# Value products of both query halves issued together, in parts of 256 columns

## The chip, the cores and the metric

The kernel runs on one core of a Trainium2 chip. The metric is the device time of one execution in microseconds. Before the change it is 2518.14 us, the median of three runs (2516.71 to 2518.36). Everything is computed in 32-bit floats: either plain fp32, or fp32r operands split by hand into an exact high part and the rest.

## The reference

A two-layer generator works on 1024 latent tokens and 256 context tokens of width 1024. Each layer modulates the stream, projects it once, feeds three groups of heads (a bidirectional recurrence, grouped attention, neighbourhood attention), gates and projects the result and normalises it. What the change touches is the attention of the two last groups, cut to what matters:

```python
# grouped attention: 6 query heads, 2 key heads, head width 64, all 256 + 1024 keys
s = jnp.einsum('bqgrd,bsgd->bgrqs', qi, keys)
p = jax.nn.softmax(s, axis=-1)
o = jnp.einsum('bgrqs,bsgd->bqgrd', p, vals)
# neighbourhood attention: 4 heads, the same with a window of 8 x 16 grid cells,
# a learned bias on the scores of the window, and all context keys in the same softmax
```

In layer 0 the context tokens attend too (to the 256 context keys); layer 1 leaves them out.

## The kernel before

`layer_proj` computes the projections of a layer, calls the recurrence (`rwkv`, through `mid`) and then the last projections; `attention(l)` comes behind it in the text, and `out_proj` behind that. The program is built with a planner (`schedule_with_timeline_sim=True`, L1369): it decides, while the program is built, in which order each engine gets its instructions, from what is ready in its own model of the run and from the order of the text. On the chip every engine then takes its instructions in that fixed order. So the recurrence, which is earlier in the text, and the attention are interleaved on all engines.

The recurrence is a serial chain of 40 steps in each layer (`wave_chain`): small matmuls at L704, a copy on ScalarE (L710), matmuls at L715, copies (L721), matmuls at L725, a product on VectorE (L730), and the next step. L630 copies a wave's transposed tiles on ScalarE, 16 copies a wave.

Attention goes head by head in pairs of loops that run side by side: `pair_main` of the current head and `pair_max` of the next. `pair_max` computes the scores of the next head once (L863, tile `sm`) and reduces each row to its maximum on VectorE (L865). `pair_main` computes the scores again, transposed, with keys on the partitions and 512 queries along them, minus the maximum (L920, L921, tile `st`, two buffers), takes their exponential on ScalarE (L927, tile `pt`, three buffers for each half) and multiplies it with the values (L909). A head has two jobs, the two halves of its 1024 queries. A step of the loop over `g` takes one key tile of 128 keys for both halves; a head of the grouped attention has ten steps. In the neighbourhood heads a step can see 256 or 384 queries, some of the other half (`split`), and a bias is added on VectorE before the exponential (L929).

A value product has 128 keys as its contraction and 64 output rows. So both halves fit side by side into TensorE's columns: half 0 has the column tile at 0, half 1 that at 64 (`tile_position=(0, 64 * i)`), and both accumulate in one PSUM tile `y` of 128 x 512, which has one buffer. Sums over keys are kept by adding the exponentials up on GpSimd and VectorE (L934). `weigh` issues the value products of the step before, kept in `todo`, behind the scores of the current step in the text. Each fp32 value product shows in the trace as two records of the same shape, one behind the other.

At the end of a head `ys` (L954) copies `y` out, the sums are inverted and the result is written to `yg_d`, which the output projection (L1141 to L1143) reads; the output blocks of the recurrence (`out_block`, L761 to L787) write there too.

## Time and profile before

| | |
|---|---|
| median of three runs | 2518.14 us |
| the profiled execution, from its first to its last instruction | 2517.7 us |
| TensorE busy | 2289.5 us, 91% |
| VectorE busy | 1669.4 us, 66% |
| GpSimd busy | 1188.4 us, 47% |
| ScalarE busy | 979.5 us, 39% |
| value products, L909 | 784 records, 343.6 us busy |

PE is TensorE's matmuls, PEld its weight loads, DVE VectorE, ACT ScalarE, POOL GpSimd, SP the queue that issues most DMAs. A row of the timeline merges neighbours of one engine that have the same line and tiles: it has the start, the length of the whole, and behind the shape the number of records (x2 is one value product, x4 two of them). A record's end is modelled and overlaps the next start; what an instruction takes from TensorE is therefore read from its start to the start of the next row. [...]

The stretches used here: neighbourhood heads from 560 to 822 us (layer 0) and 1823 to 2046 us (layer 1), grouped heads from 822 to 1197 us and 2046 to 2388 us.

### The profile page before, as it was taken

The page shows a single profiled execution, that of the slowest core. Times are in us where ns is not written, and L with a number is a line of the kernel's source. Part 1 is how long each engine was busy: PE and PEld are TensorE (multiplying, and loading weights), DVE is VectorE, ACT ScalarE, POOL GpSimd, SP SyncE. Part 2 cuts the span into 40 slices and gives each one's busy share as a digit, 9 for nine tenths or more (in the row PEclk, how much of TensorE's full clock was granted, in tenths as well). Part 3 has the DMA queues.
Part 4 walks back from the last instruction along what each step waited for, and adds up shares of the span by engine and source line. Part 5 has one row for each costly group of instructions (what it writes and reads, how often), then busy time and mean ns, then how long its engine had stood idle before and what let it go on. Part 6 is the DMA issues. An engine that isn't in the chain of part 4 may idle for free. (4 is left out here: it accounts for less than half of the span.)

```text
span 2517.7 us, 56578 instructions
## 1 busy us (share of the span) xinstructions
PE 2289.5 (91%) x22008; PEld 1601.3 (64%) x22008; DVE 1669.4 (66%) x3183; ACT 979.5 (39%) x2074; POOL 1188.4 (47%) x1438
## 2 busy tenths in 40 slices
PE   6989999978898999999899999999778889999887
PEld 3878798765455554544887777887555554544387
DVE  5685524647878878665387885445478797786646
ACT  3433413333544444444233444133344444454422
POOL 4454425344555544453355465344455545544443
PEclk9999999997889999999999999999789898999999
DMA  7355325455555444441332546245645443332332
GB/s 276 117 167 169 106 80 137 101 139 115 123 117 124 104 109 102 114 140 54 104 98 95 159 143 199 87 97 138 154 105 123 101 96 97 83 80 64 112 110 95
DMA packets 448236, 298.09 MB, mean 118 GB/s; under 512 B 249600, under 2 KB 395880, under 8 KB 446944
## 3 DMA queue, kind: packets, MB, share of 16 engines
q1 hardware_dynamic: 439936, 281.71, 41.0%
q0 software_dynamic: 7392, 10.28, 1.5%
q8 instruction: 173, 2.83, 0.5%
q10 hardware_dynamic: 640, 2.49, 0.4%
q14 instruction: 95, 0.78, 0.1%
HBM read 198.37 MB, written 91.79 MB: 115 GB/s over the span
## 5 line engine op out<-in xcount | busy, mean ns | idle before, releaser
L204 PE MATMUL pj<-hlo,wh 128*128 128x512 f32 (+1 forms) x1072 | 400.7, 374 | 14.0 <-DVE hlo L480 7.9
L203 PE MATMUL pj<-hhi,wh 128*128 128x512 f32 (+1 forms) x1072 | 402.9, 377 | 9.8 <-ACT qr L348 5.9
L205 PE MATMUL pj<-hhi,wl 128*128 128x512 f32 (+1 forms) x1072 | 398.9, 373 | 0.2 <-POOL wl L169 0.2
L909 PE MATMUL y<-pt,v 128*64 128x512 f32 (+3 forms) x784 | 343.6, 570 | 0.0
L865 DVE TENSOR_REDUCE mx<-sm 128x1 f32<-128x512 f32 (+1 forms) x372 | 200.5, 555 | 85.4 <-PE sm L863 83.3
L169 POOL TENSOR_TENSOR wl<-wf,wh 128x512 fp32r<-128x512 f32 x104 | 142.9, 1378 | 205.8 <-ACT wh L168 181.8
L204 PEld LDWEIGHTS pj<-hlo,wh 128*128 128x128 f32 x1072 | 204.2, 191 | 55.3 <-DVE hlo L480 8.2
L203 PEld LDWEIGHTS pj<-hhi,wh 128*128 128x128 f32 x1072 | 203.9, 191 | 55.5 <-ACT qr L348 7.2
L927 ACT ACTIVATE pt<-st 128x512 f32<-128x512 f32 (+1 forms) x292 | 166.7, 583 | 179.4 <-PE st L921 176.9
L205 PEld LDWEIGHTS pj<-hhi,wl 128*128 128x128 f32 x1072 | 204.0, 190 | 37.2 <-issue 2.9
L863 PE MATMUL sm<-k,q 128*128 128x256 f32 (+2 forms) x436 | 167.2, 427 | 20.8 <-DVE mx L865 13.6
L920 PE MATMUL st<-q,k 128*128 128x512 f32 (+3 forms) x376 | 166.8, 447 | 18.3 <-DVE pt L929 6.2
L863 PEld LDWEIGHTS sm<-k,q 128*128 128x128 f32 x436 | 80.3, 203 | 151.8 <-DVE mx L865 41.6
L1141 PE MATMUL pj<-yh,wh 128*128 128x256 f32 x576 | 161.2, 291 | 15.9 <-ACT yh L1115 11.8
L934 POOL TENSOR_TENSOR acc<-acc,pt 128x512 f32<-128x512 f32 x80 | 107.0, 1337 | 138.1 <-ACT pt L927 137.6
L1142 PE MATMUL pj<-yl,wh 128*128 128x256 f32 x576 | 164.4, 288 | 1.0 <-POOL yl L1116 0.9
L1143 PE MATMUL pj<-yh,wl 128*128 128x256 f32 x576 | 162.8, 287 | 0.0
L921 PE MATMUL st<-q,k 65*128 65x512 f32 (+3 forms) x376 | 147.7, 396 | 1.8 <-issue 1.1
L909 PEld LDWEIGHTS y<-pt,v 128*64 128x64 f32 x784 | 72.0, 143 | 104.8 <-issue 94.1
L616 DVE TENSOR_TENSOR G<-gt,msk 64x192 f32<-64x192 f32 (+1 forms) x320 | 110.3, 345 | 39.4 <-PE gt L611 28.0
L920 PEld LDWEIGHTS st<-q,k 128*128 128x128 f32 x376 | 74.8, 200 | 93.8 <-ACT pt L927 28.1
L699 POOL MEMSET X<- 32x192 f32 x320 | 81.7, 255 | 108.8 <-PE ch L742 84.5
(276 smaller groups left out, 5126.5 us busy)
## 6 DMA issues: line engine op xcount, KB each, us to landing
wf<-win SPq DMA_DIRECT2D x104, 256.0 KB
wm<-wmod SPq DMA_DIRECT2D x32, 512.0 KB
yf<-yg_d SPq DMA_DIRECT2D x72, 128.0 KB
wt<-wm SPq DMA_DIRECT2D x8, 1024.0 KB
gate_d<-o SPq DMA_DIRECT2D x32, 256.0 KB
wf<-wout SPq DMA_DIRECT2D x16, 512.0 KB
ldkk<-rw_d SPq DMA_DIRECT2D x40, 192.0 KB
ldkd<-rw_d SPq DMA_DIRECT2D x40, 192.0 KB
```

Of the source, the lines that this page charges most:

```text
L203: nc.tensor.matmul(out=ps[:, :n], lhsT=wh, rhs=hhi[:, k, t0:t0 + n], start=(k == 0), stop=False)
L204: nc.tensor.matmul(out=ps[:, :n], lhsT=wh, rhs=hlo[:, k, t0:t0 + n], start=False, stop=False)
L205: nc.tensor.matmul(out=ps[:, :n], lhsT=wl, rhs=hhi[:, k, t0:t0 + n], start=False, stop=(k == KT - 1))
L863: nc.tensor.matmul(out=sp_[:, :o], lhsT=q[0][:, qc:qc + 128], rhs=k[0][:, c0:c0 + o], start=True, stop=True)
L865: nc.vector.tensor_reduce(out=mx[:, n_:n_ + 1], in_=sp_[:, :o], op=ALU.max, axis=AX.X)
L909: nc.tensor.matmul(out=o, lhsT=v[:, t, :], rhs=p_, start=start, stop=stop and n_ >= len(mm) - 2, tile_position=(0, 64 * i))
L920: nc.tensor.matmul(out=o, lhsT=k[0][:, 128 * t:128 * t + 128], rhs=q[0][:, qa:qb], start=True, stop=False)
L921: nc.tensor.matmul(out=o, lhsT=k[1][0:65, 128 * t:128 * t + 128], rhs=q[1][0:65, qa:qb], start=False, stop=True)
L927: nc.scalar.activation(out=pt[:, :w], in_=sp_[:, :w], func=AF.Exp)
L1141: nc.tensor.matmul(out=p_, lhsT=wh[m][:, k], rhs=yh, start=(x_ == 0), stop=False)
L1142: nc.tensor.matmul(out=p_, lhsT=wh[m][:, k], rhs=yl, start=False, stop=False)
L1143: nc.tensor.matmul(out=p_, lhsT=wl[m][:, k], rhs=yh, start=False, stop=(x_ == KT - 1))
```

## The change

`weigh` no longer sorts the products of a step by half. It makes two lists, one for each half (column tile), cuts each product into parts of at most 256 columns, and issues the lists in turns: first part of half 0, first part of half 1, second part of half 0, and so on. A second edit gives the first of these products a dependency, for the planner's order alone (no semaphore), on the last score product of the second half in the current step (`follow`). The flags that open and close an accumulation are set for each half. Docstrings and comments are dropped.

```diff
+    def follow(ins, prev):
+        tc.add_manual_dep(ins.ins, prev.ins.name, mybir.DependencyInfo(mybir.DependencyClass.NoSync, mybir.DependencyReason.DATA), reason="order")
...
-            todo = []
+            todo, after = [], []
...
             def weigh(stop=False):
-                mm = []
-                for i, first, pt, tiles in todo:
-                    for x_, (t, cc, _) in enumerate(tiles):
+                lanes = [[], []]
+                for x_ in range(max(len(u[3]) for u in todo)):
+                    for i, first, pt, tiles in todo:
+                        t, cc, _ = tiles[x_]
                         if cc is None:
-                            mm.append((x_, i, t, y[64 * i:64 * i + 64, :nq], pt[:, nq * x_:nq * x_ + nq], first and x_ == 0))
+                            src = [(i, 0, nq, nq * x_)]
                         else:
-                            mm += [(i != h, h, t, y[64 * h:64 * h + 64, lo - 512 * h:hi - 512 * h], pt[:, lo - cc[0]:hi - cc[0]], first) for h, lo, hi in split(*cc)]
-                mm.sort(key=lambda u: u[:2])
-                for n_, (_, i, t, o, p_, start) in enumerate(mm):
-                    nc.tensor.matmul(out=o, lhsT=v[:, t, :], rhs=p_, start=start, stop=stop and n_ >= len(mm) - 2, tile_position=(0, 64 * i))
+                            src = [(h, lo - 512 * h, hi - 512 * h, lo - cc[0]) for h, lo, hi in split(*cc)]
+                        for h, c0, c1, p0 in src:
+                            for a0 in range(c0, c1, 256):
+                                a1 = min(a0 + 256, c1)
+                                lanes[h].append((t, pt, a0, a1, p0 + a0 - c0, first and not lanes[h]))
+                order = []
+                for n_ in range(max(len(z) for z in lanes)):
+                    order += [(i, n_) + z[n_] for i, z in enumerate(lanes) if n_ < len(z)]
+                for n_, (i, at, t, pt, a0, a1, p0, start) in enumerate(order):
+                    mm = nc.tensor.matmul(out=y[64 * i:64 * i + 64, a0:a1], lhsT=v[:, t, :], rhs=pt[:, p0:p0 + a1 - a0], start=start,
+                                          stop=stop and at == len(lanes[i]) - 1, tile_position=(0, 64 * i))
+                    if n_ == 0 and after:
+                        follow(mm, after.pop())
                 todo.clear()
+                after.clear()
...
-                        nc.tensor.matmul(out=o, lhsT=k[1][0:65, 128 * t:128 * t + 128], rhs=q[1][0:65, qa:qb], start=False, stop=True)
+                        mm = nc.tensor.matmul(out=o, lhsT=k[1][0:65, 128 * t:128 * t + 128], rhs=q[1][0:65, qa:qb], start=False, stop=True)
...
-                weigh()
+                    after.append(mm)
+                if todo:
+                    weigh()
```

## Rows read from the trace of the kernel before

**Rows 1.** The page's first and fourth parts: busy time of the engines, and the two lines of the chain that ended last.

```profile
PE 2289.5 (91%) x22008; PEld 1601.3 (64%) x22008; DVE 1669.4 (66%) x3183; ACT 979.5 (39%) x2074; POOL 1188.4 (47%) x1438
...
PE 23%; DVE 11%; DMA 6%; issue 3%; ACT 2%; POOL 2%; SPq 1%; DVEq 0%; POOLq 0%; ACTq 0%
...
PE y L909 4%; PE sm L863 2%; PE pj L203 1%; PE pj L204 1%; PE pj L205 1%; PE st L920 1%; PE pj L1141 1%; PE pj L1143 1%; PE pj L1142 1%; DMA yf<-yg_d 1%; DVE G L616 1%; PE st L921 1%; PE ch L725 1%; DMA ls_d<-G 1%; DMA x_d<-s 1%
```

**Rows 2.** Busy time by stretch, grouped heads of layers 0 and 1, then neighbourhood heads of layers 0 and 1. Behind the length: busy us (records) of PE, PEld, DVE, ACT, POOL; granted clock; DMA share and GB/s.

```profile
822.00:1197.00 375.00, 363.54 (x3965) 181.18 (x3962) 268.61 (x595) 171.63 (x386) 174.94 (x200) 0.97 0.39 104
2046.00:2388.00 342.00, 322.10 (x3615) 158.14 (x3615) 256.29 (x547) 156.36 (x340) 168.07 (x194) 0.97 0.34 88
560.00:822.00 262.00, 221.33 (x3143) 137.92 (x3132) 209.66 (x552) 119.97 (x293) 134.49 (x187) 0.85 0.53 122
1823.00:2046.00 223.00, 186.59 (x2843) 115.88 (x2839) 183.01 (x503) 100.56 (x238) 120.02 (x167) 0.88 0.47 106
```

**Rows 3.** The same for the value products (L909) alone: busy us (records) of PE and PEld, and the clock and DMA of the stretch.

```profile
822.00:1197.00 375.00, 134.76 (x280) 26.24 (x280) 0.97 0.39 104
2046.00:2388.00 342.00, 120.77 (x240) 21.50 (x240) 0.97 0.34 88
```

**Rows 4.** What TensorE waited for in the two stretches of grouped heads, longest first (layer 0, then layer 1 after the dots): us in total, times, longest.

```profile
PE kt L626 <- DVE tt L680: 2.3, 1, 2.3
PE ls L951 <- DVE acc L934: 2.1, 1, 2.1
...
PE sm L863 <- DVE mx L865: 3.7, 5, 1.4
PE ch L715 <- ACT rsb L710: 3.0, 3, 1.7
```

**Rows 5.** Timeline of TensorE at the end of layer 0's last grouped head, where nothing else is on it.

```profile
1191.56 1.07 PE L909 MATMUL y<-pt,v 128*64 128x512 f32 x2
1192.56 0.50 PE L920 MATMUL st<-q,k 128*128 128x512 f32 x1
1192.89 0.39 PE L921 MATMUL st<-q,k 65*128 65x512 f32 x1
1193.21 1.07 PE L909 MATMUL y<-pt,v 128*64 128x512 f32 x2
1194.22 0.50 PE L920 MATMUL st<-q,k 128*128 128x512 f32 x1
1194.56 0.39 PE L921 MATMUL st<-q,k 65*128 65x512 f32 x1
1194.88 1.08 PE L909 MATMUL y<-pt,v 128*64 128x512 f32 x4
1195.88 0.63 PE L951 MATMUL ls<-acc,onec 128*32 128x256 f32 x4
```

**Rows 6.** Timeline around the first and the last case at the full clock in which two products of 512 columns, one of each half, stand next to each other and start together (at either clock the grouped heads have 14 of these: 3 in layer 0, 11 in layer 1); PEld rows are the weight loads.

```profile
1110.45 0.20 PEld L909 LDWEIGHTS y<-pt,v 128*64 128x64 f32 x4 [0.38 <-issue]
1110.46 1.08 PE L909 MATMUL y<-pt,v 128*64 128x512 f32 x4
...
1111.47 0.27 PE L876 MATMUL mt<-c_ident,nm 128*1 128x128 f32 x1
...
2338.96 1.08 PE L909 MATMUL y<-pt,v 128*64 128x512 f32 x4
...
2339.97 0.41 PE L951 MATMUL ls<-acc,onec 128*32 128x256 f32 x2
```

**Rows 7.** Timeline of TensorE at two steps of neighbourhood heads in which both halves see 384 queries: uncut (four records of 384 columns), and cut by the boundary between the halves into parts of 256 and 128 columns (eight records).

```profile
731.51 0.87 PE L909 MATMUL y<-pt,v 128*64 128x384 f32 x4
732.30 0.39 PE L863 MATMUL sm<-k,q 128*128 128x256 f32 x1
...
1933.67 0.87 PE L909 MATMUL y<-pt,v 128*64 128x256 f32 x8
1934.47 0.50 PE L920 MATMUL st<-q,k 128*128 128x512 f32 x1
```

**Rows 8.** Timeline of TensorE with a product of 256 columns that stands alone.

```profile
622.62 0.65 PE L909 MATMUL y<-pt,v 128*64 128x256 f32 x2
623.20 0.38 PE L863 MATMUL sm<-k,q 128*128 128x256 f32 x1
```

**Rows 9.** Value products of 512 and of 384 columns in the neighbourhood heads of layer 0, then of layer 1: count | busy us, mean ns | idle.

```profile
L909 PE MATMUL y<-pt,v 128*64 128x512 f32 x32 | 17.2, 618 | 0.0
L909 PE MATMUL y<-pt,v 128*64 128x384 f32 x32 | 13.8, 572 | 0.0
...
L909 PE MATMUL y<-pt,v 128*64 128x512 f32 x32 | 14.8, 645 | 0.0
L909 PE MATMUL y<-pt,v 128*64 128x384 f32 x32 | 12.9, 512 | 0.0
```

**Rows 10.** ScalarE's timeline in layer 1, with an exponential (L927) among copies of the recurrence.

```profile
2245.89 1.29 ACT L630 COPY S<-kt 64x192 f32<-64x192 f32 x4
2247.20 0.60 ACT L927 ACTIVATE pt<-st 128x512 f32<-128x512 f32 x1
...
2248.80 1.28 ACT L630 COPY S<-kt 64x192 f32<-64x192 f32 x4
```

**Rows 11.** The recurrence's first matmuls (L704, 24 records a step) by stretch of layer 1: busy us (records) of PE and PEld.

```profile
1899.00:1974.00 75.00, 2.71 (x120) 1.91 (x120) 0.95 0.52 112
...
2124.00:2199.00 75.00, 2.72 (x120) 1.91 (x120) 0.95 0.35 86
```

**Rows 12.** TensorE's timeline where the recurrence meets little else: the first matmuls of two steps, one behind the other.

```profile
1808.96 0.87 PE L704 MATMUL ch<-X,G 128*32 128x64 f32 x24
...
1818.68 0.87 PE L704 MATMUL ch<-X,G 128*32 128x64 f32 x24 [3.36 <-DVE X L730]
```

**Rows 13.** Weight loads of the value products over the whole span: shortest, median and longest, ns; first and last start.

```profile
L909 PEld LDWEIGHTS y<-pt,v x784: 132/136/233, 584.6 to 2387.0; 128*64 128x64 f32 x196
```

## Prediction

> **What bounds the kernel now.** I read the page first: TensorE is busy 91% of the span, VectorE 66%, and the value products are the largest single line of the chain that ended last, 4% of the span [rows 1]. An average over a whole layer says little about attention, so I cut it into stretches. In the grouped heads TensorE is busy 363.5 of 375 us in layer 0 and 322.1 of 342 us in layer 1, at a granted clock of 0.97, with VectorE at 268.6 and 256.3 us [rows 2]; its longest waits there are 2.3 to 3.7 us in total [rows 4]. There TensorE sets the pace. In the neighbourhood heads it is busy 221.3 of 262 and 186.6 of 223 us, at a clock of 0.85 and 0.88, and VectorE, with 209.7 and 183.0 us, is as loaded [rows 2]: there nobody is alone the bound.
>
> The value products take 134.8 and 120.8 us of TensorE in the two grouped stretches, more than a third of what it does [rows 3]. The reader should look at how they stand. A lone product of 512 columns takes 1.00 us from its start to the next start (1191.56 to 1192.56), and a half step is 0.33 + 0.33 us of scores and this 1.00: 1.66 us, twice for each key tile [rows 5]. Where by chance two products of different halves stand next to each other, both together take 1.00 to 1.01 us: 1194.88 to 1195.88, 1110.46 to 1111.47, 2338.96 to 2339.97 [rows 5, 6]. The two column tiles work at the same time. But the order seldom lets them: 240 records in each grouped stretch (layer 0's other 40 are of context queries, 128 columns wide) are 120 products, 60 possible pairs, and only 3 and 11 pairs stand together. Half 0's scores of the next step become ready when half 0's exponential has freed their buffer, then half 0's product, then the same of half 1.
>
> **The change, part by part.** *Pairing.* Each pair brought together saves 1.00 + 1.00 - 1.01 = 0.99 us of TensorE. Layer 0: 57 x 0.99 = 56.4 us; layer 1: 49 x 0.99 = 48.5 us. In the neighbourhood heads I halve the busy time of the products of 512 and 384 columns, 31.0 us in layer 0 and 27.7 in layer 1 [rows 9]: 15.5, and 12 in layer 1, where a few already stand in pairs. The products of 128 columns I leave out. Together 132 us of TensorE.
>
> *Parts of 256 columns.* They double the products of 512 columns: 136 pairs in the program get two more products for each pair, each with weight loads. Uncut, a pair of 384 columns takes 731.51 to 732.30, 0.79 us; cut into 256 and 128 it takes 1933.67 to 1934.47, 0.80 us [rows 7]. So a pair of four parts costs 1.01 to 1.02 us; I take nothing for the cut. The upper end is a part that stands alone: 0.58 us [rows 8], four of them 2.32 us. The lower end is zero, since no column goes away. The loads themselves (median 136 ns [rows 13]) lie under the running products: four start and end within 0.20 us at the head of a pair that runs 1.08 us [rows 6].
>
> [...]
>
> *The added order.* The first product of a step now stands behind the scores of the next step's second half. Nothing but TensorE's order changes: no DMA and no instruction of SP or GpSimd is moved, and `v` and `pt` are read later, with three buffers of `pt`. What is queued behind is all of TensorE's later work. Does it stall? Let half 1's scores end at T. The pair runs until T + 1.01, half 0's next scores until T + 1.67. Half 1's next scores need half 1's exponential, 0.60 us [rows 10], ready at T + 0.62: 1.05 us to spare. ScalarE, however, runs copies of the recurrence in groups of 1.29 us in front of an exponential [rows 10], and then TensorE waits where before it had half 0's product to do. The bounds of this: nothing, or the excess of 1.29 over 1.05, 0.24 us, at every key step, 120 x 0.24 = 29 us. I don't add it by itself, since the next step counts idle time as a whole.
>
> *From TensorE's time to the span.* With less work, TensorE will wait more for the others. Rows 2 give two kinds of stretch: VectorE's busy time is 0.74 of TensorE's and the stretch is 1.03 of TensorE's (layer 0, grouped), or 0.95 and 1.18 (layer 0, neighbourhood). A line through these has a slope of 0.73; the other two stretches (0.80 with 1.06, 0.98 with 1.20) lie within 0.015 of it. With the savings: grouped layer 0, TensorE 307.1, ratio 0.875, factor 1.131: 347.4 us, 28 less. Layer 1: 273.6, 0.937, 1.176: 321.8, 20 less. Neighbourhood heads: 205.8, 1.02, 1.236: 254.4, 8 less; and 174.6, 1.05, 1.258: 219.6, 3 less. So by the line 48 us in the grouped heads. The other end is that idle time stays as it is: 105 us. I take a quarter of the way from the line to that end, 62 us, because the line's upper points are heads with an addition of VectorE in front of each exponential of the window, which the grouped heads don't have. With 11 us of the neighbourhood heads: 73 us. The profiled span is 2517.7, 0.4 below the median of the runs: 2518.1 - 73 = **2445 us**. Own range of this case 2410 to 2470 (60 to 105 with something lost, or 48).
>
> **The rivals.** *A, TensorE stays the bound throughout.* The grouped heads give all of 105 us, and the neighbourhood heads half of 27: 2518 - 118 = 2400. For it: waits of a few us in 375. Against: VectorE would have to be busy 0.84 and 0.87 of the shortened stretches.
>
> *B, the recurrence keeps its pace, or the pairs are broken up by it.* Layer 1's recurrence takes 120 records at L704 in 75 us, five steps, 15 us each, in the neighbourhood heads as in the grouped heads [rows 11], and it ends with attention. If that pace does not quicken, layer 1 gains nothing, and layer 0, whose recurrence ends earlier, its 28 to 40: about 2480. Against: with little else on TensorE a step took 9.7 us (1808.96 to 1818.68) [rows 12], so most of the 15 are queues. The recurrence is earlier in the text, so the planner may also put its matmuls between the four parts; half of the pairs lost gives 2518 - 36 = 2482. That would be the change not doing what it says.
>
> *C, slower: the clock.* Place: both grouped stretches. If waits of the new order make them like the neighbourhood heads, TensorE has a busy share of 0.845 and a clock of 0.85 there (product 0.718), 0.837 and 0.88 in layer 1 (0.736) [rows 2]. The work that is left is 307.1 x 0.97 = 297.9 and 273.6 x 0.97 = 265.4 us at full clock; divided by the products: 415 and 361 us, 40 and 19 longer than now: 2577. It decides the sign where share times clock falls below 297.9 / 375 = 0.79 and 265.4 / 342 = 0.78; now it is 0.94 and 0.91. Nothing in the profile shows so large a fall without VectorE's full load.
>
> *D, the halves don't overlap in the new order.* Four lone parts [rows 8] take 2.32 instead of 2.01 us: 136 x 0.31 = 42 us, 2560. If instead the eight weight loads of a pair were exposed (8 x 0.136 = 1.09 us on top of 1.01, 2.10 us for a pair): 136 x 0.09 = 12 us, 2530. [...] Against both: rows 6 and 7.
>
> **How the numbers follow.** The likeliest case has 0.46, A 0.15, B 0.20, no change (gains and new waits cancel) 0.05, C 0.10, D 0.04. A difference of 0.2%, 5 us, is about what a measurement of this kernel can tell from no change. Faster: 0.46 + 0.15 + 0.20 = 0.81; same 0.05; slower 0.14. The range takes in nearly all of A, B, and no change, and leaves out C, D and the edge of A: 2390 to 2518.
>
> **What would show it.** Right: in the timeline L909 in rows of x8 that run about 1.08 us, about 120 of 120 pairs in the grouped heads, and its busy time near 65 us in each of these stretches; TensorE's time falling by about 50 us in each, its idle share rising to some 10%, its clock above 0.9; the recurrence's steps near 13 us. A shows as idle time unchanged, B as steps still of 15 us, or as L909 rows split by L725 or L704, C as a clock near 0.86 in the grouped heads, D as L909 rows of more than 2 us. The prediction is wrong if the value products' time halves and the grouped stretches shrink by less than 20 us in sum, or if the pairs are not in the timeline at all.

## The result and the profile after

The changed kernel takes 2503.78 us, the median of 18 runs (2485.41 to 2518.45), against 2517.24 us (18 runs) of the kernel before beside it: a ratio of 0.994 [0.9921, 0.9959], 13.5 us or 0.6% faster. The forecast was 2445 us. The sign is right, and the size is 73 us forecast for 13.5 found.

The page of the changed kernel, its busy time of the engines, stands against [rows 1]:

```profile
PE 2204.5 (88%) x22616; PEld 1655.1 (66%) x22616; DVE 1660.7 (66%) x3183; ACT 978.7 (39%) x2074; POOL 1188.3 (47%) x1438
```

and the group of the value products, now L921, from TensorE's groups over the whole span (before: 784 records, 343.6 us at L909):

```profile
L921 PE MATMUL y<-pt,v 128*64 128x256 f32 (+1 forms) x1392 | 221.2, 406 | 2.7 <-ACT pt L943 2.3 <-issue 0.3
```

The change did what it says. The products went from 343.6 to 221.2 us of TensorE, 122.4 us less, with more and shorter records. Yet TensorE's whole busy time fell only from 2289.5 to 2204.5, by 85.0 us: all its other matmuls together take 37.4 us more than before. And the span, 2517.7 before, is 2502.0, so that TensorE's idle time rose from 228.2 to 297.5, by 69.3 us. The whole result is in this sum, -122.4 + 37.4 + 69.3 = -15.7 us of span. A group's busy time takes each record to its modelled end, which overlaps the next start. Counted from each start to the next over both traces, as rows are read here, the products go from 313.2 to 201.0 us and all other matmuls from 1976.3 to 2003.5: the same sum is then -112.2 + 27.2 + 69.3.

Busy time by stretch, in the order of [rows 2] (columns as there; the grouped heads end at 1196 and 2366 us now):

```profile
822.00:1196.00 374.00, 335.27 (x4251) 205.96 (x4252) 268.38 (x607) 173.20 (x392) 171.04 (x197) 0.91 0.41 106
2046.00:2366.00 320.00, 285.90 (x3941) 178.13 (x3941) 255.88 (x559) 156.76 (x344) 167.09 (x198) 0.93 0.37 95
560.00:822.00 262.00, 200.86 (x3252) 138.29 (x3253) 204.31 (x549) 119.41 (x288) 143.74 (x193) 0.85 0.53 124
1823.00:2046.00 223.00, 176.31 (x2842) 117.39 (x2838) 180.29 (x489) 99.06 (x236) 116.53 (x162) 0.85 0.48 108
```

The same stretches for the value products alone, to be read against [rows 3]:

```profile
822.00:1196.00 374.00, 84.15 (x528) 37.68 (x528) 0.91 0.41 106
2046.00:2366.00 320.00, 72.54 (x480) 31.90 (x480) 0.93 0.37 95
560.00:822.00 262.00, 34.73 (x208) 15.22 (x208) 0.85 0.53 124
1823.00:2046.00 223.00, 29.42 (x176) 12.27 (x176) 0.85 0.48 108
```

In the grouped heads the products fell by 50.6 and 48.2 us, in the neighbourhood heads by 13.4 and 9.7 (the same view of the kernel before has 48.1 and 39.1 us there). But layer 0's grouped heads end where they did (1197, now 1196 us). Only layer 1's end earlier, 22 us. Idle time in the two grouped stretches went from 11.5 and 19.9 to 38.7 and 34.1 us, and the granted clock from 0.97 in both to 0.91 and 0.93.

TensorE's timeline of the changed kernel shows the pair itself, first early in the tail of layer 0, then at its end, where nothing else is left (the rows are those of [rows 5]):

```profile
1094.20 1.98 PE L921 MATMUL y<-pt,v 128*64 128x256 f32 x8
1096.11 0.80 PE L867 MATMUL sm<-k,q 128*128 128x512 f32 x1
...
1183.35 1.08 PE L921 MATMUL y<-pt,v 128*64 128x256 f32 x8
1184.36 0.50 PE L936 MATMUL st<-q,k 128*128 128x512 f32 x1
...
1185.49 1.08 PE L921 MATMUL y<-pt,v 128*64 128x256 f32 x8
```

At the end a pair in four parts takes 1.01 us, 1183.35 to 1184.36, and a whole key step for both halves 2.14 us (1183.35 to 1185.49), where it took 1191.56 to 1194.88, 3.32 us [rows 5]. Here the change gives its full gain. At 1094 us the same eight records take 1.91 us, about twice as long: the granted clock of that stretch is 0.50, where it is 1.00 at the end. In both traces it has no other values; "lower level" stands for 0.50 below, and "full" for 1.00. Of the 120 pairs of the grouped heads (60 in each layer) 105 stand unbroken, with nothing between their eight records; most of the others are split into six and two.

Who ends TensorE's waits? Three groups over the whole span, first of the kernel before, then of the changed one; the last part of a row is the idle time just before the group and what ended it:

```profile
L725 PE MATMUL ch<-X,S 128*64 128x64 f32 x1920 | 87.9, 239 | 6.7 <-DVE X L721 5.6 <-DVE nm L870 0.4 <-DVE onec L816 0.4
L626 PE MATMUL kt<-c_ident,kb 128*128 128x128 f32 x240 | 45.4, 304 | 19.5 <-DVE tt L680 17.3 <-ACT S L630 2.2
L876 PE MATMUL mt<-c_ident,nm 128*1 128x128 f32 x360 | 55.1, 301 | 3.3 <-DVE nm L870 2.0 <-DVE mx L865 0.8 <-DVE mx L867 0.5
```

```profile
L725 PE MATMUL ch<-X,S 128*64 128x64 f32 x1920 | 86.0, 242 | 21.1 <-DVE X L721 20.6 <-DVE onec L820 0.4
L626 PE MATMUL kt<-c_ident,kb 128*128 128x128 f32 x240 | 48.9, 322 | 28.1 <-DVE tt L680 25.4 <-ACT S L630 2.4 <-DMA stg<-k_d 0.2
L880 PE MATMUL mt<-c_ident,nm 128*1 128x128 f32 x360 | 56.7, 300 | 17.8 <-DVE mx L869 9.9 <-DVE mx L871 6.0 <-DVE nm L874 1.9
```

The recurrence's L725 waits 21.1 us in place of 6.7 (for the VectorE copy at L721), the transposes at L626 28.1 in place of 19.5, those of the maxima (L876, now L880) 17.8 in place of 3.3. Nearly all of it is ended by VectorE. So is most of the rise in all: over the whole span, the waits of TensorE that VectorE ends go from 116.5 to 173.7 us, 57 of the 69 us. The chain of waits in one stretch, 2046 to 2360 us in layer 1, says the same; shares of the stretch by line, of the kernel before and then of the changed one:

```profile
by line: PE y L909 23.7%; PE sm L863 9.3%; PE st L920 8.7%; PE st L921 6.1%; issue 3.9%; PE ch L725 3.9%; DVE G L616 3.3%; DMA ls_d<-G 2.7%; DMA wf<-wout 2.5%; DVE mx L865 2.5%; DMA lin<-ls_d 2.1%; PE ch L715 2.0%; PE ch L704 2.0%; DVE acc 
```

```profile
by line: issue 7.6%; PE y L921 7.2%; DVE mx L869 4.9%; DMA ls_d<-G 4.8%; PE sm L867 4.4%; DVE acc L950 4.4%; PE st L936 3.5%; DMA yo<-y_d 3.5%; DVE e L646 3.0%; DVE G L616 3.0%; DMA lin<-ls_d 2.8%; PE st L937 2.7%; DMA y_d<-yst 2.3%; DVE tm
```

Before, the first four places are TensorE's, 47.8% of the stretch. After, the four TensorE lines have 17.8%, and maxima (L869), additions (L950), the recurrence's small operations (L646, L616) and its round trips through memory (`ls_d`, `lin`, `yo`, `y_d`) stand among them. No line stands out any more.

### The profile page after: what moved, and what is told of

The parts are those of the page before. It is cut to its first block, busy times and chain, and to the rows that moved or that the text cites. A ratio compares the mean times of both kernels' runs of the same rounds, so it can differ in the third digit from the quotient of the medians.

```text
span 2502.0 us, 57786 instructions
## 1 busy us (share of the span) xinstructions
PE 2204.5 (88%) x22616; PEld 1655.1 (66%) x22616; DVE 1660.7 (66%) x3183; ACT 978.7 (39%) x2074; POOL 1188.3 (47%) x1438
## 4 chain that ended last, share of the span: by engine, by line
PE 47%; DVE 21%; DMA 14%; issue 6%; ACT 5%; SPq 4%; POOL 3%; DVEq 0%; POOLq 0%; ACTq 0%
PE pj L203 5%; PE pj L204 5%; PE pj L205 5%; PE y L921 4%; DMA ls_d<-G 3%; PE sm L867 2%; PE st L936 2%; DVE mx L869 2%; DVE e L646 2%; DMA lin<-ls_d 2%; PE pj L1159 2%; PE st L937 2%; DVE G L616 2%; PE pj L1161 2%; PE pj L1160 2%
## 5 line engine op out<-in xcount | busy, mean ns | idle before, releaser
L203 PE MATMUL pj<-hhi,wh 128*128 128x512 f32 (+1 forms) x1072 | 404.9, 380 | 7.4 <-ACT qr L348 4.7
L203 PEld LDWEIGHTS pj<-hhi,wh 128*128 128x128 f32 x1072 | 205.0, 192 | 52.8 <-issue 7.0
L869 DVE TENSOR_REDUCE mx<-sm 128x1 f32<-128x512 f32 (+1 forms) x372 | 198.9, 553 | 39.2 <-PE sm L867 37.5
L921 PE MATMUL y<-pt,v 128*64 128x256 f32 (+1 forms) x1392 | 221.2, 406 | 2.7 <-ACT pt L943 2.3
L936 PE MATMUL st<-q,k 128*128 128x512 f32 (+3 forms) x376 | 168.0, 451 | 22.6 <-DVE am L110 6.5
L867 PE MATMUL sm<-k,q 128*128 128x256 f32 (+2 forms) x436 | 169.7, 432 | 19.5 <-DVE mx L869 7.8
L921 PEld LDWEIGHTS y<-pt,v 128*64 128x64 f32 x1392 | 97.1, 146 | 96.3 <-issue 66.3
L950 POOL TENSOR_TENSOR acc<-acc,pt 128x512 f32<-128x512 f32 x80 | 104.5, 1306 | 116.5 <-ACT pt L943 109.9
L867 PEld LDWEIGHTS sm<-k,q 128*128 128x128 f32 x436 | 84.8, 210 | 81.6 <-issue 21.0
L616 DVE TENSOR_TENSOR G<-gt,msk 64x192 f32<-64x192 f32 (+1 forms) x320 | 110.5, 345 | 39.6 <-PE gt L611 28.7
L699 POOL MEMSET X<- 32x192 f32 x320 | 82.9, 259 | 93.2 <-PE ch L742 68.8
L630 ACT COPY S<-kt 64x192 f32<-64x192 f32 x320 | 100.4, 314 | 55.4 <-PE ch L725 28.7
```

Of the source, the lines that this page charges most:

```text
L203: nc.tensor.matmul(out=ps[:, :n], lhsT=wh, rhs=hhi[:, k, t0:t0 + n], start=(k == 0), stop=False)
L867: nc.tensor.matmul(out=sp_[:, :o], lhsT=q[0][:, qc:qc + 128], rhs=k[0][:, c0:c0 + o], start=True, stop=True)
L869: nc.vector.tensor_reduce(out=mx[:, n_:n_ + 1], in_=sp_[:, :o], op=ALU.max, axis=AX.X)
L921: mm = nc.tensor.matmul(out=y[64 * i:64 * i + 64, a0:a1], lhsT=v[:, t, :], rhs=pt[:, p0:p0 + a1 - a0], start=start, stop=stop and at == le ...
L936: nc.tensor.matmul(out=o, lhsT=k[0][:, 128 * t:128 * t + 128], rhs=q[0][:, qa:qb], start=True, stop=False)
```

## The experiments

Eighteen kernels were run, each beside the kernel before on the same chip. "Ratio" is always to that.

**The parts of the change: the cut and the order.** First, the changed kernel with parts of 512 columns:

```diff
-                            for a0 in range(c0, c1, 256):
-                                a1 = min(a0 + 256, c1)
+                            for a0 in range(c0, c1, 512):
+                                a1 = min(a0 + 512, c1)
```

> The changed kernel with uncut products (parts of 512 columns), pairs and added order kept. The changed kernel's profile has the gain of TensorE (value products 343.6 to 221.2 us busy) and a span only 16 us shorter. Theory 1 (the recurrence's chain through all queues sets the pace of the interleaved stretches, the cut costs nothing): time as the changed kernel, 2497 to 2510 us. Theory 2 (the four parts and their loads cost what the pairing gains): 30 us or more faster than the changed kernel, below 2475. Value products busy 220 us or less by both.

2498.13 us, ratio 0.9933 [0.9907, 0.9959], products 222.5 us busy. The cut neither costs nor brings anything that can be told from 0.994. Then the changed kernel without the added order:

```diff
-                    if n_ == 0 and after:
-                        follow(mm, after.pop())
```

> The changed kernel without the added order; the parts still alternate. Theory 1 (recurrence sets the pace): within 10 us of the changed kernel, 2494 to 2514 us, although TensorE has the first part of half 0 alone in most steps (value products near 270 us busy, 50 more). Theory 2b (the added order makes TensorE wait for the second exponential and so gives the gain back): 20 us or more faster than the changed kernel, below 2484.

2525.44 us, ratio 1.0042 [1.0018, 1.0067], slower than before. Its value products:

```profile
L921 PE MATMUL y<-pt,v 128*64 128x256 f32 (+1 forms) x1392 | 285.1, 400 | 3.1 <-issue 1.2 <-ACT pt L944 1.0 <-ACT pt L941 0.8
```

285.1 us in place of 221.2: without the order most first parts of half 0 stand alone. In its grouped heads 20 of the 120 pairs stand unbroken (105 in the changed kernel), and most of the others are split into two and six records. The order is a part of the gain, worth 22 us by the medians (2525.4 against 2503.8), 26 by the ratios. Neither theory had expected this: Theory 1 said the same time within 10 us, Theory 2b a faster kernel.

**What pairing is worth with the recurrence out of the way.** In both kernels the recurrence is left out, and zeros are stored in its place:

```diff
     def rwkv(l, lay):
+        if True:
+            with tc.tile_pool(name=f"zf{l}", bufs=1, side="right") as zp:
...
+                for i in range(3):
+                    nc.sync.dma_start(out=yg_d[i], in_=zf)
+            return
```

> The kernel before with the recurrence left out (its gated output is replaced by zeros; its inputs are still projected). It is the base for the next run. TensorE's work of the recurrence in attention (some 200 us in sum) goes, so both theories expect 2200 to 2330 us, with attention stretches bound by TensorE, busy over 0.93.

> The changed kernel with the recurrence left out in the same way. Theory 1 (in the whole kernel the recurrence's chain takes the gain): here the pairing gives most of what was predicted of TensorE, 80 to 130 us less than the kernel before without recurrence. Theory 2 (attention itself doesn't get faster: exponentials, VectorE's maxima and sums or the clock take the gain): less than 40 us less.

2056.61 us without pairing (ratio 0.8182 [0.8151, 0.8212]) and 1934.65 with it (0.7696 [0.7672, 0.7721]): pairing is worth 122 us. Busy time in the attention of layers 0 and 1, columns as in [rows 2], first without pairing, then with it:

```profile
528.00:981.00 453.00, 432.53 (x1863) 190.64 (x1863) 238.71 (x550) 171.24 (x330) 139.53 (x105) 0.93 0.26 69
1560.00:1934.00 374.00, 361.58 (x1288) 148.40 (x1288) 211.06 (x471) 145.88 (x250) 129.07 (x94) 0.98 0.20 53
```

```profile
526.00:905.00 379.00, 354.18 (x2163) 200.37 (x2163) 252.38 (x550) 169.51 (x330) 139.28 (x105) 0.93 0.32 82
1482.00:1808.00 326.00, 302.28 (x1592) 166.67 (x1592) 235.26 (x471) 143.41 (x250) 128.74 (x95) 0.92 0.24 61
```

TensorE is idle 20 and 12 us without pairing, 25 and 24 us with it: here the time that TensorE saves is the time that the kernel saves. So the pairs are right, and it is the company of the recurrence that takes the gain. That company is more than one thing: without the recurrence VectorE too is busy only 53 and 56% of these stretches (238.7 of 453 us, 211.1 of 374), against 75 and 78% with it (the rows of whole attention below).

**Is it the length of the recurrence's serial chain?** Each step copies `rsb` on ScalarE. Moved to VectorE, in both kernels:

```diff
-                nc.scalar.copy(rsb, rs)
+                nc.vector.tensor_copy(rsb, rs)
```

> The changed kernel with one step of the recurrence's chain (the copy rsb, L710) moved from ScalarE to VectorE. In the changed kernel this copy waits 2.2 to 2.6 us a step in ScalarE's queue, and VectorE's wait in the same chain is 0.9 to 1.1 us. Theory 1 (the chain's own length through the queues is the bound of the interleaved stretches): 1.2 us of some 70 steps, 25 to 85 us less than the changed kernel. Theory 3 (the order that the planner fixed, and with it the mixture, is the bound, no single hop): within 12 us of it.

> The same move in the kernel before, where TensorE is busy 97% of the grouped heads. Theory 1: TensorE is the bound there, so the shorter chain gives less than 15 us. Theory 3: within 12 us too.

and the chain made longer, with the copy done twice on ScalarE:

```diff
-                nc.scalar.copy(rsb, rs)
+                rsa = r2.tile([128, 3, 64], F32, tag="rsa", name="rsa")
+                nc.scalar.copy(rsa, rs)
+                nc.scalar.copy(rsb, rsa)
```

> The changed kernel with the chain made longer: rsb is copied twice, one behind the other on ScalarE, about 0.3 us a step and 25 us in 80 steps. Theory 1: 12 to 35 us more than the changed kernel. Theory 3: less than 8 us more, since ScalarE is busy below half.

> The same longer chain in the kernel before. Theory 1: TensorE is the bound, so less of the 25 us shows than in the changed kernel, 0 to 12 us. Theory 3: less than 8 us.

Changed kernel: 2502.46 (0.9968 [0.9947, 0.9989]) with the copy moved, 2494.12 (0.9938 [0.9915, 0.9962]) with it doubled. The kernel before: 2545.16 (1.0139 [1.0111, 1.0167]) and 2532.89 (1.0083 [1.0059, 1.0108]). A longer chain does not slow the changed kernel: the theory that the chain's own length is the bound fell. Something else showed: small edits make the kernel before 0.8 to 1.4% slower, and leave the changed one where it is.

**VectorE relieved.** The largest item of VectorE is the maxima. They were taken over a quarter of the columns, in both kernels:

```diff
-                            nc.vector.tensor_reduce(out=mx[:, n_:n_ + 1], in_=sp_[:, :o], op=ALU.max, axis=AX.X)
+                            nc.vector.tensor_reduce(out=mx[:, n_:n_ + 1], in_=sp_[:, :o // 4], op=ALU.max, axis=AX.X)
...
-                        nc.scalar.activation(out=pt[:, :w], in_=sp_[:, :w], func=AF.Exp)
+                        nc.scalar.activation(out=pt[:, :w], in_=sp_[:, :w], func=AF.Exp, scale=1.0 / 64)
```

> The kernel before, with each row maximum of a score tile taken over the first quarter of its columns (the exponential is scaled by 1/64, so that it stays finite; the values of the output are not the reference's). VectorE loses work and nothing else changes: the reductions of L865, some 0.55 us each now, should come near 0.25 us (the 3-column reduction that follows takes 0.15), about 370 x 0.3 = 110 us of VectorE in the two attention stretches. Theory V (in the changed kernel VectorE's queue is what TensorE waits for; in the kernel before TensorE was the bound in the grouped heads): little here, 0 to 25 us less than before (2492 to 2517). Theory W (not VectorE's load, but the recurrence's preparation, a chain of round trips through all engines and two DMAs, in an order fixed at build time): also little, 0 to 25 us.

> The same edit in the changed kernel. Theory V: now TensorE waits less, and the pairing pays: at least 40 us under the changed kernel (2464 or less), and at least 60 us under the same edit in the kernel before. Theory W: as little as there, and the pair with and without pairing differs by what the three pairs so far differ by, 13 to 43 us.

VectorE's groups in layer 1's attention (busy us, mean ns), first of the changed kernel, then the maxima of this one:

```profile
L869 DVE TENSOR_REDUCE mx<-sm 128x1 f32<-128x512 f32 (+1 forms) x176 | 95.8, 561 | 16.9 <-PE sm L867 16.1
L646 DVE TENSOR_TENSOR e<-e,tmp 128x15 f32<-128x15 f32 (+7 forms) x105 | 36.6, 349 | 1.5
L644 DVE TENSOR_TENSOR tmp<-nn,e 128x15 f32<-128x15 f32 (+7 forms) x105 | 26.9, 256 | 1.7
```

```profile
L869 DVE TENSOR_REDUCE mx<-sm 128x1 f32<-128x128 f32 (+1 forms) x176 | 40.8, 252 | 21.8 <-PE sm L867 20.9
```

A reduction went from 561 to 252 ns. The kernel before became slower, 2544.99 (1.0148 [1.0116, 1.018]); the changed one went to 2455.63 (0.9802 [0.9758, 0.9845]), 35 us under its plain form by the ratios. Now pairing is worth 89 us by the medians, 87 by the ratios. This is beyond the 13 to 43 of Theory W, and over the 60 that Theory V asked for. But 37 of the 87 are the kernel before's own loss, where both theories had expected it 0 to 25 us faster; what made it slower was not found. The pages, before and after pairing:

```profile
PE 2281.7 (90%) x22008; PEld 1607.3 (63%) x22008; DVE 1560.9 (61%) x3183; ACT 979.8 (39%) x2074; POOL 1180.0 (46%) x1438
```

```profile
PE 2188.5 (89%) x22616; PEld 1643.3 (67%) x22616; DVE 1570.6 (64%) x3183; ACT 976.5 (40%) x2074; POOL 1183.5 (48%) x1438
```

TensorE's busy time differs by 93.2 us and the span (2539.3, 2454.5) by 84.8: only 8.4 us went into idle time. Next, the loop of small inverses (L644, L646) cut from 15 rounds to 1:

```diff
-            for j in range(15):
+            for j in range(1):
```

> The changed kernel with the loop of the 16x16 inverses cut from 15 rounds to 1 (28 of 30 small VectorE operations per wave left out, 7 to 12 us of VectorE and 17 to 36 us of each wave's preparation; the inverses are then wrong, so the output is not the reference's). Theory W: the recurrence gets faster, since its preparation is the chain that is late: steps of 12 us or less in place of 15, and the time falls by 50 us or more (2450 or less). Theory V: like half of the relief of the maxima, 10 to 30 us less (2474 to 2494). A third, that only the build's order counts: no fall beyond 10 us.

> The kernel before with the loop of the 16x16 inverses cut from 15 rounds to 1, the control of e12 (outputs wrong, since the inverses are). If TensorE is the bound here, as the prediction read it, little changes: 2490 to 2520, and pairing under this relief is worth 45 to 75 us. If the recurrence's preparation is late in the kernel before as well, the time falls as e12 did from the changed kernel (some 50 us, to 2460), and pairing is worth the 13 us of the plain pair again.

Changed kernel 2446.99 (0.9754 [0.9727, 0.9781]), 47 us under its plain form; the kernel before 2508.31 (0.9974 [0.9952, 0.9995]), 7 us. So the same VectorE work costs several times as much once the products are paired (47 us against 7, by the interval 1 to 12). It also meets what W expected of the changed kernel (2450 or less): this work lies in the recurrence's preparation, and e12's time alone does not tell VectorE's load from that chain. The sign that W named, steps of 12 us or less, did not come: over layer 1's attention a step of the recurrence takes 14.1 us on average, 15.3 in the changed kernel. The maxima (e10) are no part of that chain. Both reliefs together:

> The changed kernel with both reliefs of VectorE, the maxima over a quarter of the columns and the inverse's loop cut (output not the reference's). If VectorE's work is what the changed kernel waits for, both add up, and the time falls to 2420 or less; if the two took away the same wait, or the fixed order of the build is all that counts, it stays at 2440 to 2460.

> The kernel before with both reliefs. By the theory that TensorE bounds it: no lower than 2490, so that pairing is worth 80 us or more when VectorE is out of the way, on the way to the 122 us that it was worth without the recurrence. By the rival (preparation late in both kernels): 2430 or less, and pairing worth under 40 us.

2409.26 (0.9588 [0.9545, 0.9631]) and 2478.08 (0.9843 [0.9808, 0.9877]). They add up in the changed kernel (35 + 47 us by the ratios, together 89). The three reliefs take 90, 130 and 222 us off VectorE's busy time, so that each microsecond of VectorE gives 0.36 to 0.40 us of time, whichever work it is. The kernel before fell further than expected (2490 or more): once both are out, it gains too, and pairing is worth 69 us by the medians, not the 80 or more that had been expected.

All pairs side by side, from the profiled executions (busy and idle time of TensorE, span) and the runs. "Idle" is span less busy time, each column the kernel with pairing less the one without; the last column is the difference of the two ratios:

| edit in both kernels | TensorE busy | TensorE idle | span | by the ratios of the runs |
|---|---|---|---|---|
| none | -85.0 | +69.3 | -15.7 | -0.6% |
| inverse in blocks (below) | -106.2 | +67.4 | -38.8 | -1.3% |
| copy `rsb` doubled | -95.0 | +68.3 | -26.7 | -1.5% |
| copy `rsb` on VectorE | -89.5 | +52.3 | -37.2 | -1.7% |
| inverse loop cut | -111.7 | +49.1 | -62.6 | -2.2% |
| maxima and inverse loop | -99.1 | +28.5 | -70.6 | -2.6% |
| maxima over a quarter | -93.2 | +8.4 | -84.8 | -3.5% |
| no recurrence | -139.9 | +14.1 | -125.8 | -4.9% |

Pairing always takes 85 to 140 us from TensorE. With all the work of the recurrence and of VectorE in place, 52 to 69 us of it come back as idle time; with VectorE relieved, 8 to 49. The rows do not follow the amount of VectorE work taken away: with both reliefs pairing is worth less than with the maxima alone, since the kernel before loses with the one and gains with the two.

**Versions meant to beat both.** Every second addition of half 1 on GpSimd, then this with uncut products:

```diff
-                    eng = nc.vector if i or end else nc.gpsimd
+                    eng = nc.vector if end or (i and g % 2) else nc.gpsimd
```

> The changed kernel with every second addition of half 1's exponentials (L950) moved from VectorE (0.83 to 0.94 us) to GpSimd (1.31 us): 30 or so per layer, 25 us less VectorE work and 40 us more GpSimd work in each layer. Theory V: 5 to 20 us under the changed kernel (2484 to 2499). Theory W: no difference (within 5 us), or a little slower, since GpSimd also zeroes the recurrence's operands.

> A version meant to beat both: the changed order with uncut products (e1) and every second addition of half 1's exponentials on GpSimd (e11). If the two small gains are real and add up, 2485 to 2495 (ratio 0.988 to 0.993 to the kernel before); if they were differences of the build's order, anywhere from 2485 to 2510.

2497.78 (0.9955 [0.9927, 0.9984]) and 2506.17 (0.9962 [0.9934, 0.9991]): neither can be told from the changed kernel (0.994), and the two do not add up. VectorE's busy time hardly fell (1656.5 against 1660.7 us): 56 additions left it, and others of its operations got longer (last section). So it was no relief, and no test of Theory V. Last, the inverse in 20 operations in place of 30, in both kernels (its core):

```diff
-            for j in range(15):
-                n = 15 - j
+            for j in range(7):
+                n = 7 - j
...
+            nc.vector.tensor_tensor(out=pr, in0=ap(e, 136, (16, 8), (0, 8), (1, 8)), in1=ap(tmp_, 0, (0, 8), (1, 8), (8, 8)), op=ALU.mult)
+            nc.vector.tensor_reduce(out=e[:, 8:16, 0:8], in_=pr, op=ALU.add, axis=AX.X, negate=True)
```

> A version meant to beat both that computes the same: in the changed kernel each 16x16 inverse is made from two 8x8 inverses at once (7 rounds of two operations) and a product for the lower left block (three multiplications and three sums), 20 VectorE operations in a chain in place of 30. Cutting the loop to 2 operations took 48 us from the changed kernel, so by that measure 10 of 28 operations should give 48 x 10/28 = 17 us: about 0.987 of the kernel before (2480 where the changed kernel has 2497). If only the operations' busy time counts (some 7.2 us per wave, here about 6): 5 us or nothing that can be told.

> The same in the kernel before. There the cut loop (e13) gave 4 us; by that measure 2 us, ratio 0.999, within what can be told from none. Paired with e17 this gives a fifth measure of the pairing: 15 us more than the plain pair's 13 if VectorE's chain is what the changed kernel waits for, the same 13 if not.

2502.3 (0.9938 [0.9915, 0.9962]) and 2534.18 (1.0067 [1.0043, 1.0091]): the 17 us did not come. Its VectorE groups in layer 1's attention:

```profile
L649 DVE TENSOR_TENSOR e<-e,tmp 128x14 f32<-128x14 f32 (+3 forms) x49 | 11.2, 228 | 1.1
L647 DVE TENSOR_TENSOR tmp<-nn,e 128x14 f32<-128x14 f32 (+3 forms) x49 | 10.3, 210 | 1.0
L656 DVE TENSOR_TENSOR nn<-e,tmp 128x512 f32<-128x512 f32 x7 | 9.7, 1379 | 0.1
L653 DVE TENSOR_TENSOR nn<-nn,e 128x256 f32<-128x256 f32 x14 | 9.6, 683 | 0.3
L657 DVE TENSOR_REDUCE e<-nn 128x64 f32<-128x512 f32 x7 | 4.7, 673 | 0.0
L654 DVE TENSOR_REDUCE tmp<-nn 128x32 f32<-128x256 f32 x14 | 5.8, 415 | 0.2
```

Seven waves take 51.3 us by these rows, where the loop took 63.5 (36.6 + 26.9): 12 us less in the whole of a layer's attention. The fewer operations are longer, the product of 512 elements 1.38 us. Counting operations, as the expectation did, was the mistake: over the whole span VectorE is busy 6 us less (1654.4), which at 0.36 to 0.40 us each is worth 2 to 3. The pair of e17 and e18 gives 1.3%, 32 us, near the 28 of the expectation, but only because the kernel before got slower. No version was found that is clearly faster than the changed kernel and computes the same.

## Why the prediction was right in sign and wrong in size

*Pairing* was right, and somewhat too large: 132 us of TensorE forecast, 122.4 found as busy time, 112.2 from start to start. By stretch, as busy time, 50.6 for 56.4 and 48.2 for 48.5 in the grouped heads, 13.4 for 15.5 and 9.7 for 12 in the others; from start to start, as the forecast counted its 0.99 us a pair, the grouped heads gave 46.4 and 42.4. *The parts of 256 columns* cost nothing, as said (e1). Rival D put a pair at 2.32 us if the halves did not overlap, and at 2.10 us if its eight weight loads were exposed; it takes 1.01 with eight weight loads (1183.35 to 1184.36). Rival D fell with that.

*The added order* was forecast at a cost of 0 to 29 us. It is the other way round: e2 shows that without it the pairs break, and 22 to 26 us are lost.

*From TensorE's time to the span* is the step that failed. The sum took 132 us off TensorE and gave 59 back as idle time: 73. The trace gives -122.4 and +69.3 (-112.2 and +69.3 from start to start), so these two terms were off by 10 to 20 us and by 10, and a third, 27 to 37 us, was in no term at all: the other matmuls got slower. The granted clock over the span fell from 0.949 to 0.926. I had weighed the clock as an all-or-nothing rival (C, 0.10) of 59 us; it came by degrees, with the time at the lower level (0.50) going from 256 to 369 us of the span. The two traces show that the clock, and not the company of other matmuls, accounts for this term. From start to start, the other matmuls take 178.7 us at the lower level before and 261.7 after. Set against the mean of the same line and shape at the full level of the kernel before, that is 78 us too long before and 112 after, 34 more; what they take at the full level differs by 6 us the other way. At the same level a record takes the same in both kernels: the first projection (L203) 241 and 240 ns at the full one, 460 and 455 at the lower.

The line through the four stretches, and the choice to go a quarter beyond it, treated each stretch as if its length followed from two busy times. In layer 1 the length came out, the line saying 20 us and the grouped stretch becoming 22 shorter, but by luck: TensorE is busy 285.9 us there where the line took 273.6, and idle 34.1 where it gave 48.2. In layer 0 it said 28, and the stretch became 1 shorter. Its idle time is near what the line gave (38.7 us, 40.3 forecast); its busy time is not, 335.3 us for 307.1. From start to start the products fell 46.4 us there, 10 less than forecast, and the other matmuls rose by 18.1, their time at the lower level going from 14.8 to 46.6 us. The recurrence, which is not last in that layer, also got ahead of attention; that this adds to the miss is not shown. The transposed scores (L920, then L936) issued until its last step begins, and behind it, by the kernel before and by the changed one (busy us and records):

```profile
560.00:1103.00 543.00, 68.76 (x164) 33.13 (x164) 0.91 0.47 113
1103.00:1198.00 95.00, 20.03 (x44) 8.47 (x44) 0.96 0.32 102
```

```profile
560.00:1078.00 518.00, 63.13 (x148) 30.39 (x148) 0.89 0.49 116
1078.00:1196.00 118.00, 27.34 (x60) 12.49 (x60) 0.87 0.33 103
```

The last step begins 25 us earlier, at 1078 instead of 1103, but 60 half steps of attention are left over instead of 44. Over both layers the attention stretches, whole, went like this (before, then after; columns as in [rows 2]):

```profile
566.00:1198.00 632.00, 584.36 (x7033) 318.05 (x7033) 476.16 (x1145) 289.54 (x677) 306.81 (x386) 0.92 0.44 110
1824.00:2388.00 564.00, 507.68 (x6447) 273.35 (x6447) 438.30 (x1049) 256.40 (x577) 287.14 (x360) 0.93 0.39 96
```

```profile
574.00:1196.00 622.00, 531.16 (x7333) 339.89 (x7336) 465.91 (x1145) 288.84 (x676) 308.01 (x385) 0.89 0.45 112
1825.00:2366.00 541.00, 460.20 (x6747) 294.03 (x6747) 434.25 (x1042) 255.78 (x580) 283.16 (x359) 0.90 0.41 100
```

Together 33 us shorter, of which the span keeps 15.7: attention starts 8 us later in layer 0, 3 us go between the layers (1198 to 1824, 1196 to 1825), and 6 behind the last (129.7 us to the end, now 136.0).

*Rival B* (0.20, 2480 us) is the nearest to the time, for partly wrong reasons: it had layer 0 gain 28 to 40 us and layer 1 nothing, and it went the other way. The recurrence's first matmuls in the two windows of [rows 11]:

```profile
1899.00:1974.00 75.00, 2.57 (x96) 1.76 (x96) 0.93 0.50 108
2124.00:2199.00 75.00, 3.62 (x120) 2.42 (x120) 0.93 0.42 97
```

96 and 120 records are four and five steps in 75 us: about the 15 us of before, where the forecast had 13. That is not because its chain of states is rigid (e5 and e7). Each of its hops stands in the fixed order of three engines among attention's work (in both traces VectorE's 3183 records come line for line in the order of the program), and what TensorE waits for is mostly VectorE (173.7 of 285 us of its waits): making VectorE's work shorter gave 35 us (e10), 47 (e12) and 89 (e14) in the changed kernel, and in the one before a loss (e9), 7 (e13) and 40 (e15). *Rival A* fell: with VectorE at 0.80 of TensorE's busy time in layer 0's grouped heads and 0.89 in layer 1's, idle time there went from 31.4 to 72.8 us.

Of what would show it, the value products' time "near 65 us" in each grouped stretch was 84 and 73, the clock above 0.9 held, and the idle share is 10 and 11%. The test that I gave for being wrong, under 20 us from the grouped stretches, was just missed with 23; it says little about the whole time, since the starts moved.

Open is how much of the small gain belongs to the order that the planner happened to find for the kernel before. Its neighbours with small edits (e6, e8, e18) are 0.7 to 1.4% slower, one with 100 us less VectorE work is 1.5% slower (e9), while those of the changed kernel stay within 0.993 and 0.997. In the four pairs with all work in place, pairing gives 0.6, 1.3, 1.5 and 1.7%: the plain pair is the lowest of them. What in the order makes it so was not found.

## What to carry to other kernels

Time taken from the busiest engine was worth nearly its own size here where no second engine was close behind: without the recurrence, with VectorE at 0.55 and 0.58 of TensorE's busy time in attention, 139.9 us less of TensorE gave 125.8 us of span. With the recurrence in place, VectorE at 0.74 to 0.80 of TensorE's load in the grouped heads and interleaved with it in a fixed order, idle time took back more than half (69 of 112 to 122 us, 57 of them ended by VectorE), and slower matmuls at a granted clock of 0.50 a quarter to a third (27 to 37). Before forecasting such a gain, leave the other party out (here the recurrence: 122 us) and relieve the next engine in both kernels (89 us): the pairs of runs tell a lost gain from a wrong mechanism. Where a planner fixes the order, one kernel against one other is a sample of one, and two or three small edits of both show how far it scatters (0.7 to 1.4% here).

## What the runs showed of the hardware

The granted clock fell with TensorE still busy most of the time. The tail of layer 0 behind the recurrence's last step, of the changed kernel and of the one before (columns as in [rows 2]):

```profile
1078.00:1196.00 118.00, 109.66 (x730) 61.84 (x731) 78.07 (x137) 55.40 (x107) 51.20 (x37) 0.87 0.33 103
```

```profile
1103.00:1198.00 95.00, 92.75 (x458) 39.18 (x446) 59.95 (x105) 44.51 (x86) 39.49 (x26) 0.96 0.32 102
```

TensorE is busy 93% of it at a clock of 0.87, where it was 98% and 0.96. Where the granted clock is 0.50, a pair takes 1.91 us (1094.20 to 1096.11) instead of 1.01 where it is 1.00 (1183.35 to 1184.36).

VectorE's addition of 512 columns is not one price in these runs. In layer 0's attention without the recurrence, the same group without pairing and with it:

```profile
L941 DVE TENSOR_TENSOR acc<-acc,pt 128x512 f32<-128x512 f32 x56 | 47.7, 853 | 25.6 <-ACT pt L934 25.1 <-DVE gtl L987 0.2
```

```profile
L957 DVE TENSOR_TENSOR acc<-acc,pt 128x512 f32<-128x512 f32 x56 | 64.8, 1169 | 24.2 <-ACT pt L950 23.6
```

853 and 1169 ns for the same shape. The traces show what goes with it, as far as GpSimd's spans in them are exact. With no GpSimd instruction beside it, the addition takes 687 ns without pairing and 689 with it; with one beside it for some of its time, 1204 and 1436. Without pairing 38 of the 56 additions run with none beside them, with pairing 20. That pairing brings the exponentials of both halves, which the two engines add up, closer together would explain this, but is not shown. And where additions went to GpSimd (e11), the inverse's small operations, which no edit touched, got longer; over the whole span, of the changed kernel and then of e11:

```profile
L646 DVE TENSOR_TENSOR e<-e,tmp 128x15 f32<-128x15 f32 (+2 forms) x300 | 93.4, 311 | 6.3
L644 DVE TENSOR_TENSOR tmp<-nn,e 128x15 f32<-128x15 f32 (+2 forms) x300 | 77.5, 258 | 6.9 <-DVE nn L636 0.5
```

```profile
L646 DVE TENSOR_TENSOR e<-e,tmp 128x15 f32<-128x15 f32 (+2 forms) x300 | 101.9, 340 | 6.8
L644 DVE TENSOR_TENSOR tmp<-nn,e 128x15 f32<-128x15 f32 (+2 forms) x300 | 85.2, 284 | 6.9
```

311 to 340 and 258 to 284 ns. Here too the same operations take 204 or 205 ns in both kernels with no GpSimd instruction beside them; beside one, those of L646 take 575 and 597 ns on average, and in e11 103 of the 300 do, in place of 86. The maxima (L869) hardly change, 529 ns without and 568 beside GpSimd. The 16.2 us that L646 and L644 took more are part of why VectorE's busy time fell by only 4.2 us in e11 (1660.7 to 1656.5), where 56 additions left it.
